# Expert stage of a fused block: gate buffers laid out by blocks of tokens, one gate block built in each step, early inner products split on GpSimd beside the sorting or made from raw weights

## The chip, the cores and the metric

The kernel runs on one core of a Trainium2 chip. A core has five engines that work side by side, each with a queue of its own that it takes in order: TensorE (PE, matrix products, its weight loads shown apart as PEld), VectorE (DVE), ScalarE (ACT), GpSimd (POOL) and SyncE (SP, which issues most of the transfers). The metric is the device time of one execution in microseconds, lower is better. The kernel before takes 1970.99 us, the median of three runs that lie between 1969.98 and 1974.43.

## The reference, cut to what matters

The whole is three layers of a small transformer on 256 tokens of width 1024. The change lies in one stage of it, the expert layer at the end of the first block: 16384 experts, each a row of `u` and a row of `v`. Eight heads choose 16 experts each for every token; a chosen expert gives `gelu(h . u[e]) * g * v[e]`.

```python
q = (hf @ w_q).reshape(n, PEER_HEADS, 2, PEER_HALF)
sc = jnp.einsum('nhcd,hckd->nhck', q, sub_keys)
s_top, i_top = lax.top_k(sc, PEER_TOPK)
cand_s = s_top[:, :, 0, :, None] + s_top[:, :, 1, None, :]
cand_i = i_top[:, :, 0, :, None] * PEER_N_KEYS + i_top[:, :, 1, None, :]
best_s, pos = lax.top_k(cand_s, PEER_TOPK)        # over the 16 x 16 pairs
best_i = jnp.take_along_axis(cand_i, pos, axis=-1)
g = jax.nn.softmax(best_s, axis=-1)
a = jnp.einsum('cd,ced->ce', hc, u[ic])
a = jax.nn.gelu(a, approximate=False) * gc
return jnp.einsum('ce,ced->cd', a, v[ic])
```

All is float32.

## The kernel before, in words

**Products from split weights.** A float32 weight comes from HBM in chunks of 1 MB (`load_ahead`, three buffers called raw). A chunk is cut into pieces of 128 x 1024, and each piece is split into a high and a low part in the format float32r: ACT rounds raw to hi (L287), and another engine subtracts, lo = raw - hi (L289). That engine is VectorE, or GpSimd where the plan says so. `mm3` (L320 to L322) then makes a product as three fast ones: hi x hi, hi x lo, lo x hi. Pieces are split in the order of a plan written out in `plan_peer`, three ahead of their use. There are five buffers each of hi and lo.

**The expert stage** does not gather. It computes all 16384 inner products for all 256 tokens, and multiplies them with a dense table of gates that is zero wherever an expert was not chosen. It goes over 64 steps, `ip`, each with two columns of 128 experts:

- `up(ip)` (from L871): 16 products against the normed input `xT`, split, 128 x 256 each (48 matmuls), then Gelu on ACT (L881) into a buffer `gl`.
- `down(...)`: the gated values times a 1 MB chunk of `v`, 24 matmuls of 128 x 512 each step, all added up in four PSUM banks `po`. Ahead of it a multiply with the gates (L1037, VectorE), a rounding (L1039, ACT) and a difference (L1041, VectorE) give gh and glo.

**The order of the stage.** First the input is normed, transposed and split (`Norm.finish`, `pair`; L385, L386), and the queries (`w_pq`, bank psb) and their scores against the sub-keys (pssc) are made. Then for each tile `t` of 128 tokens comes the sorting on VectorE: `top16` on 16 lists (L919 to L923), the sums of candidate pairs (L933 to L937), `top16` on those; then small operations on 128 x 128 elements that turn positions into pairs of indices (`tu`, `tb`, `fc`, `ab`; L944 to L955), one-hot sums (`eq`, L961 to L966), and the gates IJ (L973). PE transposes IJ (psij, L978), and VectorE casts the result to float16 (`IT`, `JT`, `gT`; L980 to L987).

**The table of gates** is made in quarters of 32 expert columns, in two buffers of [128, 32, 256] by turns. `build(q, n0)` makes 16 tokens of quarter q: one-hot factors on VectorE (oj L997, ei L999, og L1002 twice), 16 matmuls into a bank psg (L1008, twice eight), and for each half of eight tokens a scaled copy on ACT (L1010) and a scaled addition on VectorE (L1011) into the buffer. Their destination is `gates[...][:, :, tokens]` read as (tokens, columns), so neighbouring elements are written 1 KB apart.

**What runs where.** `LEAD` = 20 up-products are made before the main loop: five in the sorting of tile 0, six in that of tile 1, nine beside the 16 builds of quarter 0 (`UPS`). All their 40 pieces have GpSimd for the difference. The first `EARLY` = 10 keep their Gelu results in the second gate buffer, which is free until then; therefore quarter 1 can't be built before step 10, and its 16 builds are packed into steps 10 to 15. Quarters 2 and 3 get one build a step in steps 16 to 47. The other 44 up-products are made in steps 12 to 55, eight steps ahead (`KEEP`).

Apart from the places that fix an order, a scheduler arranges the instructions of each engine at compile time, close to the order of the program.

Of the kernel before, what the change touches and what calls it, by code (L numbers as in the profile page):

```python
# [34 lines left out]
NQ = 4  # L35
# [4 lines left out]
GLO = 2.0 ** 26  # L40
LEAD = 20
UPS = (0, 5, 11)
EARLY = 10
KEEP = LEAD - EARLY - 2
QI = 128 // NQ
# [133 lines left out]
def block_kernel(ctx: ExitStack, tc: tile.TileContext, a: dict, out: bass.AP, start=0, stop=99):  # L179
# [45 lines left out]
    def rsqrt(y, x, mul, add, n):  # L225
        """y = (x * mul + add) ** -0.5"""
# [18 lines left out]

    def plan_chunk(name, off, n, size, eng=None, pieces=None):
        """append pieces of the chunk at off of a weight to the order in which weights are used"""
# [24 lines left out]
            # the first one in parts, to begin with what is there  # L272
# [6 lines left out]
    def split_ahead(upto):  # L279
        """splits pieces of the plan into float32r high and low parts up to the given one"""  # L280
        while done["part"] < min(upto + 1, len(plan)):
# [3 lines left out]
            r = raws[name, off][:, i * size:i * size + w]  # L285
            hi = whi.tile([128, 1024], F32R, name="hi")
            A.activation(out=hi[:, :w], in_=r, func=AF.Copy)  # L287
            lo = wlo.tile([128, 1024], F32R, name="lo")
            eng.tensor_tensor(out=lo[:, :w], in0=r, in1=hi[:, :w].bitcast(F32), op=OP.subtract)  # L289
# [5 lines left out]
    def weights(name, off, ahead=AHEAD):  # L295
        """accessor of a chunk: (column, width) -> high and low parts"""

        def get(c0, n):
# [5 lines left out]
            return hi[:, o:o + n], lo[:, o:o + n]  # L304
# [83 lines left out]
    def transpose_split(src, nk, name, gain=None, pool=None):  # L388
        """src: [128, 2, nk*128] tokens on partitions -> hi, lo [128, nk, 256]"""
# [18 lines left out]
    class Prep:  # L408
        """transposed halves of the residual times a gain, unscaled; the reciprocal root mean square of the tokens apart"""
# [10 lines left out]
        def pair(self, k0):  # L420
# [25 lines left out]
    class Norm(Prep):  # L446
        """scaled before the transposition, which waits for the whole"""
# [5 lines left out]
        def finish(self, pool):  # L453
# [11 lines left out]
    def take(make):  # L465
        """what the stage before has begun, or all of it now"""
# [6 lines left out]
    def begun(make, n):  # L473
        """chunk n of the residual is final: on with what the next stage does to it first"""
# [12 lines left out]
    def ends(nxt, f=add_resid):  # L487
        """consumer of a last product: f, and the beginning of the next stage behind it"""
# [11 lines left out]
    def to_rows(r, pool, name, bank=bank):  # L500
        """[128, 2] per token -> [128, 256], the same on all partitions; made at the first use"""
# [19 lines left out]
    def sin_of(dst, ang, shift, pool, n, nm):  # L521
        """dst = sin(ang + shift * 2 pi), shift in turns; ang [P, n]"""
# [34 lines left out]
    def causal_softmax(pool, ps, nk, bias, scale, e_out, sums):  # L557
        """ps [128, nk] psum scores; e_out [128, nk]; sums [128, 1]"""
# [8 lines left out]
    def transpose_p(pool, p0, p1, name="pT", bank=bank):  # L567
        """p0 [128, 128] (queries 0..127), p1 [128, 256] -> [128, 384]: keys 0..127 x 256 queries, keys 128..255 x queries 128..255"""
# [8 lines left out]
    # ------------------------------------------------------------------ mixing  # L577
# [11 lines left out]
    def mem_kv(p1):  # L589
        """keys and values of the memory"""  # L590
# [23 lines left out]
    def stage_mix():  # L614
        x = prep_mix()
        # in this order: the first products wait for it
# [11 lines left out]
        with ExitStack() as es:  # L628
# [60 lines left out]
            # indexer and selection  # L689
# [21 lines left out]
            # differential attention  # L711
# [40 lines left out]
            # sparse attention  # L752
# [26 lines left out]
            # gates, memory, output  # L779
# [1177 lines left out]
```

## Time and profile before

| | |
|---|---|
| median of three runs | 1970.99 us |
| span of the profiled execution | 1970.1 us |
| PE busy | 1870.6 us, 95% |
| DVE busy | 1464.1 us, 74% |
| ACT busy | 998.0 us, 51% |
| POOL busy | 172.6 us, 9% |
| chain of waits that ended last | PE 82%, DVE 14% |

In the profile a row of a group reads: line, engine, operation, output<-inputs, sizes, count | busy us, mean ns of one | idle time of the engine ahead of it, and what ended that. A row of the timeline reads: start, length, engine, line, operation, count, and in brackets the idle time ahead and what ended it. A row by stretches reads: stretch, its length, busy time of each engine with its number of instructions, granted clock of TensorE, share of the DMA engines, GB/s. Rows of instructions that follow each other overlap a little, and matmuls overlap each other much, so that the distance of their starts is what counts.

### The profile page before, as it was taken

To read this page: it belongs to the slowest core of one execution; us is meant where nothing else is said; L and a number is where in the kernel's file an instruction comes from. 1 tells how busy PE (TensorE), PEld (TensorE's weight loads), DVE (VectorE), ACT (ScalarE), POOL (GpSimd) and SP (SyncE) were. 2 spreads that over 40 slices of the span, in tenths; PEclk is the share of its full clock that TensorE was granted. 3 is DMA by queue.
4 is the path that set the end of the run, shared out by engine and by line. 5 is a ranking of instruction groups with operands and counts; after the bars stand their busy time and mean duration, and the time that the engine had idled before them with its cause. 6 is when DMAs were issued, how large, how long until landed. Compare 5 with 4: busy or idle time off the path is not lost.

```text
span 1970.1 us, 31681 instructions
## 1 busy us (share of the span) xinstructions
PE 1870.6 (95%) x12512; PEld 1659.4 (84%) x12512; DVE 1464.1 (74%) x2893; ACT 998.0 (51%) x1549; POOL 172.6 (9%) x223
## 2 busy tenths in 40 slices
PE   8999989657999999999999999999999999999997
PEld 6777879656878999999999888898899989699996
DVE  7786668999889977887765578641777788677777
ACT  6566456334555555555554454433444466654445
POOL 0000006444000000000000101223000000000000
PEclk9999989878999999999999999998999999999999
DMA  7433424232534555554455544200355545155552
GB/s 275 170 141 112 166 87 157 99 107 86 182 139 152 181 181 175 191 179 172 174 190 184 183 165 147 86 1 12 136 180 193 182 162 180 50 184 193 193 172 96
DMA packets 43766, 296.32 MB, mean 150 GB/s; under 512 B 4897, under 2 KB 5041, under 8 KB 10209
## 3 DMA queue, kind: packets, MB, share of 16 engines
q1 hardware_dynamic: 41872, 289.35, 41.6%
q0 software_dynamic: 1184, 3.89, 0.6%
q8 instruction: 98, 1.61, 0.3%
q10 hardware_dynamic: 560, 1.05, 0.1%
q14 instruction: 52, 0.42, 0.1%
HBM read 293.23 MB, written 1.05 MB: 149 GB/s over the span
## 4 chain that ended last, share of the span: by engine, by line
PE 82%; DVE 14%; ACT 2%; issue 1%; DMA 0%; SPq 0%; ACTq 0%; DVEq 0%
PE po L320 6%; PE po L322 6%; PE po L321 5%; PE psa L321 4%; PE psa L322 4%; PE psa L320 4%; PE psf L320 4%; PE psf L322 4%; PE psf L321 4%; PE acc L321 4%; PE acc L320 4%; PE acc L322 4%; PE psb L320 2%; PE psb L322 2%; PE psb L321 2%; PE go L322 2%
## 5 line engine op out<-in xcount | busy, mean ns | idle before, releaser
L287 ACT ACTIVATE hi<-raw 128x1024 fp32r<-128x1024 f32 (+2 forms) x551 | 575.7, 1047 | 595.3 <-PE psa L321 197.8
L289 DVE TENSOR_TENSOR lo<-raw,hi 128x1024 fp32r<-128x1024 f32 (+3 forms) x511 | 616.7, 1209 | 238.3 <-ACT hi L287 237.7
L322 PE MATMUL psa<-xTh,lo 128*128 128x256 f32 x1024 | 295.0, 288 | 1.9 <-POOL lo L289 1.9
L320 PE MATMUL psa<-xTh,hi 128*128 128x256 f32 x1024 | 295.2, 288 | 0.8 <-ACT hi L287 0.8
L321 PE MATMUL psa<-xTl,hi 128*128 128x256 f32 x1024 | 295.3, 288 | 0.0
L320 PE MATMUL po<-hi,gh 128*128 128x512 f32 x512 | 206.1, 403 | 0.0
L320 PEld LDWEIGHTS psa<-xTh,hi 128*128 128x128 f32 x1024 | 201.5, 197 | 3.0 <-ACT hi L287 1.0
L322 PEld LDWEIGHTS psa<-xTh,lo 128*128 128x128 f32 x1024 | 201.4, 197 | 2.3 <-POOL lo L289 2.1
L321 PEld LDWEIGHTS psa<-xTl,hi 128*128 128x128 f32 x1024 | 201.5, 197 | 1.9
L322 PE MATMUL po<-hi,glo 128*128 128x512 f32 x512 | 202.8, 397 | 0.1
L321 PE MATMUL po<-lo,gh 128*128 128x512 f32 x512 | 202.5, 395 | 0.0
L320 PE MATMUL psf<-xTh,hi 128*128 128x256 f32 x704 | 199.4, 283 | 0.0
L321 PE MATMUL psf<-xTl,hi 128*128 128x256 f32 x704 | 199.2, 283 | 0.0
L322 PE MATMUL psf<-xTh,lo 128*128 128x256 f32 x704 | 198.9, 283 | 0.0
L321 PEld LDWEIGHTS psf<-xTl,hi 128*128 128x128 f32 x704 | 134.6, 191 | 1.8
L320 PEld LDWEIGHTS psf<-xTh,hi 128*128 128x128 f32 x704 | 134.6, 191 | 1.7
L322 PEld LDWEIGHTS psf<-xTh,lo 128*128 128x128 f32 x704 | 134.7, 191 | 0.1
L322 PEld LDWEIGHTS po<-hi,glo 128*128 128x128 f32 x512 | 97.0, 190 | 23.1 <-DVE glo L1041 0.5
L321 PEld LDWEIGHTS po<-lo,gh 128*128 128x128 f32 x512 | 96.8, 189 | 20.2
L320 PEld LDWEIGHTS po<-hi,gh 128*128 128x128 f32 x512 | 96.9, 189 | 20.0
L289 POOL TENSOR_TENSOR lo<-raw,hi 128x1024 fp32r<-128x1024 f32 x40 | 99.5, 2502 | 131.9 <-ACT hi L287 128.6
L321 PE MATMUL acc<-lo,xTh 128*128 128x512 f32 (+3 forms) x288 | 111.0, 385 | 0.0
(635 smaller groups left out, 3690.2 us busy)
## 6 DMA issues: line engine op xcount, KB each, us to landing
raw<-in_u_dram SPq DMA_DIRECT2D x64, 1024.0 KB, 4.8
raw<-in_v_dram SPq DMA_DIRECT2D x64, 1024.0 KB, 4.8
raw<-in_w_f_dram SPq DMA_DIRECT2D x44, 1024.0 KB, 4.9
raw<-in_w_fo_dram SPq DMA_DIRECT2D x22, 1024.0 KB, 4.9
raw<-in_w_in_dram SPq DMA_DIRECT2D x17, 1024.0 KB, 4.8
raw<-in_w_pg_dram SPq DMA_DIRECT2D x8, 1024.0 KB, 4.9
raw<-in_w_hr_dram SPq DMA_DIRECT2D x6, 1024.0 KB, 4.8
raw<-in_w_out_dram SPq DMA_DIRECT2D x4, 1024.0 KB, 4.7
```

Source lines behind the costliest of these rows:

```text
L287: A.activation(out=hi[:, :w], in_=r, func=AF.Copy)
L289: eng.tensor_tensor(out=lo[:, :w], in0=r, in1=hi[:, :w].bitcast(F32), op=OP.subtract)
L320: T.matmul(ps, l[0], r[0], start=first, stop=False, skip_group_check=not check)
L321: T.matmul(ps, l[0], r[1], start=False, stop=False, skip_group_check=not check)
L322: T.matmul(ps, l[1], r[0], start=False, stop=last, skip_group_check=not check)
```

## The change

- Both gate buffers are laid out as [128, 16 blocks, 32 columns, 16 tokens]. Inside a block the tokens of a column lie side by side, so L1010 and L1011 now write runs of eight, and read PSUM with a step of 64 elements (256 bytes) between neighbours.
- Block b of the second buffer holds the Gelu result of up-product b until step b. `EARLY` goes from 10 to 14: blocks 14 and 15 are free from the start, and block b is free after step b. So quarter 1 is built at one block a step in steps 0 to 15, as quarters 2 and 3 are.
- Ten of the 20 early up-products, 5, 6 and 12 to 19 (`RAW`), are made from raw weights: 16 plain float32 matmuls against `x32`, a float32 copy of the normed input, in place of 48. Their pieces are not split at all. `x32` is filled in `pair` by ACT, eight copies more at the start of the stage. Its place is later taken by `gx`, the pairs gh and glo.
- `UPS` becomes (0, 7, 14): seven up-products beside each tile's sorting, six (all raw) beside the builds of quarter 0.
- The first GpSimd split that is planned after the sorting of tile 0 has been written out waits for the last small cast of that tile (`gate`).
- `SLOTS` = 9 Gelu buffers instead of 10, `KEEP` = 7 steps ahead instead of 8; up-products 20, 21 and 22 come in steps 4, 8 and 12, the others in steps 16 to 56 (`UP_AT`).
- The one-hot tensors `irep` and `eq` have one buffer in place of two; `irep` lies in the place of the queries.

```diff
-UPS = (0, 5, 11)
-EARLY = 10
-KEEP = LEAD - EARLY - 2
+UPS = (0, 7, 14)
+RAW = {5, 6, 12, 13, 14, 15, 16, 17, 18, 19}
+EARLY = 14
+SLOTS = 9
+KEEP = SLOTS - 2
+UP_AT = {4 * (n - LEAD) + 4: [n] for n in range(LEAD, EARLY + SLOTS)}
+UP_AT.update({n - KEEP: [n] for n in range(EARLY + SLOTS, 64)})
...
 def split_ahead(upto):
...
+            if eng == "raw":
+                parts[done["part"]] = r, None
+                chunks["left"][name, off] -= 1
+                done["part"] += 1
+                continue
...
-            eng.tensor_tensor(out=lo[:, :w], in0=r, in1=hi[:, :w].bitcast(F32), op=OP.subtract)
+            ins = eng.tensor_tensor(out=lo[:, :w], in0=r, in1=hi[:, :w].bitcast(F32), op=OP.subtract)
+            if eng is G and gate:
+                tc.add_manual_dep(ins.ins, gate.pop().name, mybir.DependencyInfo(mybir.DependencyClass.Sync, mybir.DependencyReason.DATA), reason="pause")
...
 def pair(self, k0):
...
+                if self.full is not None:
+                    A.activation(out=self.full[:, k0 + j, :], in_=ps[:, j * 256:(j + 1) * 256], func=AF.Copy, scale=self.gain(k0 + j))
...
-            gelu_p = es.enter_context(pool("pegl", LEAD - EARLY))
-            gates = [None, p0.tile([128, QI, 256], F32, name="gate1")]
+            gelu_p = es.enter_context(pool("pegl", SLOTS))
+            gates = [None, p0.tile([128, NB, QI, 256 // NB], F32, name="gate1")]
+            x32 = p0.tile([128, 8, 256], F32, name="x32", tag="x32")
...
-                        mm3(ps[:, m * 256:(m + 1) * 256], uw((m * 8 + k) * 128, 128),
-                            (xT[0][:, k, :], xT[1][:, k, :]), k == 0, k == 7)
+                        w = uw((m * 8 + k) * 128, 128)
+                        if ip in RAW:
+                            T.matmul(ps[:, m * 256:(m + 1) * 256], w[0], x32[:, k, :], start=k == 0, stop=k == 7)
+                        else:
+                            mm3(ps[:, m * 256:(m + 1) * 256], w, (xT[0][:, k, :], xT[1][:, k, :]), k == 0, k == 7)
...
-                    V.tensor_scalar(out=gT[1][:, ts], in0=gf, scalar1=GLO / GHI, scalar2=None, op0=OP.mult)
+                    small = V.tensor_scalar(out=gT[1][:, ts], in0=gf, scalar1=GLO / GHI, scalar2=None, op0=OP.mult)
+                    if t == 0:
+                        gate.append(small.ins)
...
-                    d = gates[q % 2][:, :, n0 + b * nb:n0 + (b + 1) * nb].rearrange("p i n -> p n i")
-                    A.activation(out=d, in_=ps[:, :, 0], func=AF.Copy, scale=1.0 / GHI)
-                    V.scalar_tensor_tensor(out=d, in0=ps[:, :, 1], scalar=1.0 / GLO, in1=d, op0=OP.mult, op1=OP.add)
+                    d = gates[q % 2][:, n0 // NB, :, b * nb:(b + 1) * nb]
+                    A.activation(out=d, in_=ps[:, :, 0].rearrange("p n i -> p i n"), func=AF.Copy, scale=1.0 / GHI)
+                    V.scalar_tensor_tensor(out=d, in0=ps[:, :, 1].rearrange("p n i -> p i n"), scalar=1.0 / GLO, in1=d, op0=OP.mult, op1=OP.add)
...
+            gx = p0.tile([128, 2, 2, 2, 256], F32R, name="gx", tag="x32")
             for ip in range(NP):
-                if LEAD <= ip + KEEP < NP:
-                    up(ip + KEEP)
+                for n in UP_AT.get(ip, ()):
+                    up(n)
                 q, i0 = divmod(2 * ip, QI)
                 if q + 1 < NQ:
-                    f0 = EARLY if q == 0 else 0
-                    b0, b1 = (max(0, x - f0) * 16 // (16 - f0) for x in (i0 // 2, i0 // 2 + 1))
-                    for b in range(b0, b1):
-                        build(q + 1, b * NB)
+                    build(q + 1, (ip + EARLY) % NB * NB if q == 0 else ip % NB * NB)
...
-                V.tensor_tensor(out=g, in0=g, in1=gates[q % 2][:, i0:i0 + 2, :], op=OP.mult)
-                gh = ge.tile([128, 2, 256], F32R, name="gh", tag="gh")
+                g4 = g.rearrange("p m (b n) -> p m b n", b=NB)
+                V.tensor_tensor(out=g4, in0=g4, in1=gates[q % 2][:, :, i0:i0 + 2, :].rearrange("p b i n -> p i b n"), op=OP.mult)
+                gh, glo = gx[:, ip % 2, 0], gx[:, ip % 2, 1]
...
-            plan_chunk("u", ip * 128 * 2048, 2048, 1024, G)
+            plan_chunk("u", ip * 128 * 2048, 2048, 1024, "raw" if ip in RAW else G)
```

More of the change, by code (lines that the diff above doesn't have):

```diff
@@ L244, in block_kernel @@
     done = {"raw": 0, "part": 0}
+    gate = []
     def plan_chunk(name, off, n, size, eng=None, pieces=None):
@@ L303, in get @@
             hi, lo = parts[p]
-            return hi[:, o:o + n], lo[:, o:o + n]
+            return hi[:, o:o + n], lo[:, o:o + n] if lo is not None else None
         return get
@@ L408, in block_kernel @@
     class Prep:
+        full = None
         def __init__(self, gain, src=None, bank=bank, pool=hT):
@@ L451, in chunk, with finish @@
                 self.square(t, n)
-        def finish(self, pool):
+        def finish(self, pool, full):
+            self.full = full
             r = self.rstd()
@@ L885, in stage_peer @@
                 p1 = es2.enter_context(pool("pe1", 1))
-                p2 = es2.enter_context(pool("pe2", 2))
-                xT = take(prep_peer).finish(p1)
+                xT = take(prep_peer).finish(p1, x32)
                 sk = p1.tile([128, 8, 128], F32, name="sk")
@@ L891, in stage_peer @@
                 V.tensor_copy(ia, iof[:, 0:16].unsqueeze(2).to_broadcast([128, 16, 16]))
-                qT = p1.tile([128, 8, 256], F32, name="pqT")
+                qT = p1.tile([128, 8, 256], F32, name="pqT", tag="pqT")
                 scs = [p1.tile([128, 2, 8, 128], F32, name=f"psc{t}", tag=("xs", "psc1")[t]) for t in range(2)]
@@ L956, in stage_peer @@
                     IJ = p1.tile([128, 3, 8, 16], F32, name="IJ", tag="IJ")
+                    irep = p1.tile([128, 2, 8, 16, 16], BF, name="irep", tag="pqT")
                     for c in range(2):
-                        rp_ = p2.tile([128, 8, 16, 16], BF, name="irep", tag="irep")
+                        rp_ = irep[:, c]
                         A.copy(out=rp_, in_=ib[:, c].unsqueeze(3).to_broadcast([128, 8, 16, 16]))
-                        eq = p2.tile([128, 8, 16, 16], BF, name="eq", tag="eq")
+                        eq = p1.tile([128, 8, 16, 16], BF, name="eq", tag="eq")
                         V.tensor_tensor(out=eq, in0=ab[:, c].rearrange("p (h s) -> p h s", s=16).unsqueeze(2).to_broadcast([128, 8, 16, 16]),
@@ L986, in stage_peer @@
                     V.tensor_tensor(out=gf, in0=gf, in1=gT[0][:, ts], op=OP.subtract)
-                    V.tensor_scalar(out=gT[1][:, ts], in0=gf, scalar1=GLO / GHI, scalar2=None, op0=OP.mult)
+                    small = V.tensor_scalar(out=gT[1][:, ts], in0=gf, scalar1=GLO / GHI, scalar2=None, op0=OP.mult)
+                    if t == 0:
+                        gate.append(small.ins)
             oh = es.enter_context(pool("peo", 2))
-            ge = es.enter_context(pool("pee", 2))
             gp = es.enter_context(pool("peg", 1))
-            gates[0] = gp.tile([128, QI, 256], F32, name="gate0")
+            gates[0] = gp.tile([128, NB, QI, 256 // NB], F32, name="gate0")
             def build(q, n0):
@@ L1047, in stage_peer @@
                     tail.pop()
-            last = ends(lambda: Both(gates[0][:, 0:4, :].rearrange("p a n -> p (a n)")))
+            last = ends(lambda: Both(gates[0][:, 0:2].rearrange("p b i n -> p (b i n)")))
             for hf in range(2):
@@ L1882, in plan_peer @@
         for ip in range(LEAD):
-            plan_chunk("u", ip * 128 * 2048, 2048, 1024, G)
+            plan_chunk("u", ip * 128 * 2048, 2048, 1024, "raw" if ip in RAW else G)
         for ip in range(64):
-            if LEAD <= ip + KEEP < 64:
-                plan_chunk("u", (ip + KEEP) * 128 * 2048, 2048, 1024)
+            for n in UP_AT.get(ip, ()):
+                plan_chunk("u", n * 128 * 2048, 2048, 1024)
             plan_chunk("v", ip * 128 * 2048, 2048, 1024)
```

5 lines of the change are left out of this document (2 added, 3 removed).

## The prediction

> **What bounds the kernel now.** I read the profile page first, then the busy time by stretches of the expert stage, then the timelines of VectorE (DVE), GpSimd (POOL) and TensorE (PE) inside those stretches.
>
> ```profile
> span 1970.1 us, 31681 instructions
> ...
> core 0: us, PE busy (x) PEld busy (x) DVE busy (x) ACT busy (x) POOL busy (x), PEclk, DMA share, GB/s
> 320.00:366.00 46.00, 31.97 (x252) 31.45 (x251) 46.00 (x176) 21.14 (x22) 24.37 (x11) 0.85 0.32 115
> 366.00:415.40 49.40, 32.56 (x245) 31.63 (x244) 48.53 (x178) 19.76 (x22) 26.07 (x11) 0.83 0.36 129
> 415.40:495.40 80.00, 60.15 (x596) 57.98 (x596) 74.32 (x102) 34.52 (x53) 35.21 (x13) 0.87 0.26 88
> 505.60:561.40 55.80, 55.80 (x242) 45.06 (x241) 37.88 (x43) 26.44 (x31) 0.00 (x0) 1.00 0.53 189
> 561.40:637.50 76.10, 68.92 (x593) 58.59 (x593) 73.55 (x110) 41.75 (x61) 0.00 (x0) 0.98 0.39 139
> 637.50:1150.90 513.40, 513.29 (x3577) 461.45 (x3577) 380.26 (x467) 262.02 (x332) 10.47 (x31) 1.00 0.51 179
> ```
>
> The rows are, in order: sorting of token tile 0, sorting of tile 1, the 16 builds of gate quarter 0, steps 0 to 9 of the main loop, steps 10 to 15 (in which all of quarter 1 is built), steps 16 to the end. PE is full in steps 0 to 9 and from step 16 on. DVE is full, and PE idle for a quarter to a third, in the three stretches before the loop, and again in steps 10 to 15. So the stage has two kinds of time: 569 us that only less PE work would shorten, and 252 us that are DVE's. POOL is busy in just the first three rows.
>
> ```profile
> 356.45 0.69 PE L978 MATMUL psij<-ident,IJ 128*128 128x128 f32 x2 [13.54 <-DVE IJ L966]
> ...
> 412.46 0.69 PE L978 MATMUL psij<-ident,IJ 128*128 128x128 f32 x2 [13.84 <-DVE IJ L966]
> ...
> 330.13 19.04 POOL L289 TENSOR_TENSOR lo<-raw,hi 128x1024 fp32r<-128x1024 f32 x8 [6.73 <-ACT hi L287]
> ...
> 332.62 2.45 DVE L944 TENSOR_SCALAR tu<-pu 128x128 uint32<-128x128 uint32 x1
> ...
> 349.17 0.21 DVE L955 TENSOR_TENSOR ab<-ab,fc 128x128 bf16<-128x128 bf16 x1
> ...
> 357.31 0.27 DVE L973 TENSOR_TENSOR IJ<-gd,gs 128x128 f32<-128x128 f32 x1
> ...
> 364.67 1.25 DVE L985 CAST gT<-gf 128x128 f16<-128x128 f32 x1
> ...
> 366.51 2.29 DVE L987 TENSOR_SCALAR gT<-gf 128x128 f16<-128x128 f32 x1
> ...
> 388.60 2.40 DVE L944 TENSOR_SCALAR tu<-pu 128x128 uint32<-128x128 uint32 x1
> ...
> 405.04 0.21 DVE L953 TENSOR_TENSOR ab<-ab,fc 128x128 bf16<-128x128 bf16 x1
> 405.17 0.21 DVE L955 TENSOR_TENSOR ab<-ab,fc 128x128 bf16<-128x128 bf16 x1
> ...
> 415.39 1.22 DVE L997 TENSOR_TENSOR oj<-JT,io 128x2048 f16<-128x2048 f16 x1
> ```
>
> Each tile's sorting ends in small operations (L944 to L955), whose results PE waits for, 13.5 and 13.8 us. Operations of 128 elements take 2.3 to 2.45 us there, the length of one GpSimd split (19.04/8 = 2.38). The same kind takes 0.21 us the moment POOL's eight splits end, at 349.17. DVE is not working in these rows; it waits its turn behind each GpSimd split. Seven operations pay: 332.62 to 349.17 in tile 0 and 388.60 to 405.04 in tile 1, 16.5 us each, which without splits beside them are 7 x 0.2 = 1.4.
>
> **The builds** pay too. By line, busy time in the builds of quarter 0, then in a stretch of the main loop without GpSimd (oj first, then og):
>
> ```profile
> 415.39:495.43 80.04, 25.16 (x17) 0.87 0.26 88
> 700.00:800.00 100.00, 10.83 (x9) 1.00 0.51 180
> ...
> 415.39:495.43 80.04, 24.32 (x34) 0.87 0.26 88
> 700.00:800.00 100.00, 6.02 (x16) 1.00 0.51 180
> ```
>
> oj: 25.16 - 17 x 1.203 = 4.7 us lost; og: 24.32 - 34 x 0.376 = 11.5. Together 16.
>
> **The change, part by part.** Prices on PE first: one split up-product (48 matmuls), ten down-products (240), and plain float32 matmuls of 256 columns, which the raw products will be made of.
>
> ```profile
> 577.20:582.96 5.76, 5.72 (x48) 5.70 (x48) 0.00 (x0) 1.00 0.80 313
> ...
> 505.60:561.30 55.70, 55.67 (x240) 45.06 (x240) 0.00 (x0) 1.00 0.53 189
> ...
> 261.61 1.90 PE L847 MATMUL mo<-mpT,mv 128*128 128x256 f32 x8
> ```
>
> A split product is 5.76 us, a down step 5.57. The eight float32 matmuls start 1.9/8 = 0.22 to 0.24 us apart, so a raw product (16) is 3.5 us, and one raw product saves 2.3 us of PE.
>
> The Trainium skill (FP8 and Floating Point Precision, section TensorE Precision Notes) has true float32 as four passes through the array. By that the raw products would be no cheaper than the split ones, and the row just quoted, at about two passes' worth, speaks against it; the sum goes by the row, the other price is the second rival.
>
> *Start of the stage.* Eight more ACT copies (x32) stand between the eight hi parts that the query products wait for:
>
> ```profile
> 282.34 2.33 ACT L385 ACTIVATE xTh<-pst,cols 128x256 fp32r<-128x256 f32 x6 [0.17 <-PE pst L425]
> ...
> raw<-in_u_dram SPq DMA_DIRECT2D x64, 1024.0 KB, 4.8
> ```
>
> 0.39 us each, 3.1 in all; the first 48 products run on half of the parts and hide most. I take +1 (0 to 3).
>
> *Tile 0.* Products 0 to 4 still split on GpSimd, 5 and 6 are raw. Of the eight splits in a row, three (the rest of 3 and 4) still run, until about 337.3. Splits for product 7 need the buffer that product 4 frees: 337.3 + 4.8 landing + about 1 for ACT = 343, so DVE has some 6 us alone. Two or three splits then meet the one-hot operations behind. I keep four collisions of 2.25 us: of 15.1 in the seven operations and 3 at L985 and L987, 9 go, 9 stay (bounds: 0 to 18 go). PE: products 0 to 4 ended at 356.45 - 13.54 = 342.9; +1, and two raw (7.0) give 351; DVE's IJ comes at 357.3 + 1 - 7 = 351. Neither waits long.
>
> *Tile 1.* A new wait holds GpSimd's split queue until the last small cast of tile 0 (L987). Behind it are seven splits, of products 8 to 11, and nothing else; PE's products wait for them. The cast comes at about 360 (9 us behind IJ as before, its collision gone), so the seven end at 360 + 7 x 2.4 = 377. Between IJ and the small operations lay 388.6 - 357.6 = 31 us; without 3 us of collisions at the casts they begin 28 behind 351, at 379. All 15.1 us go (bounds: 0 and 15.1). PE: from 352.5, five split (28.8) and two raw (7) products: 388.3, where DVE's IJ comes at about 389 (379 + 1.4 + the 8 us from 349.2 to 357.3 in tile 0). Raw products hold one of three load buffers until PE has read it: the load for product 8 waits for product 5 (347.5) and lands with 4.8 at 352, six us ahead of its use. The builds begin at 415.4 + 1 - 9 - 15.1 = 392.3.
>
> *Builds of quarter 0.* No GpSimd split is left: 80.0 - 16 = 64. PE has six raw products in it, 21 us, hidden in the quarter of the stretch that it idles and in the three split products' worth that it no longer makes; their loads, ten us apart, hide as well. The pair gh and glo takes the place of x32, so the first rounding waits for the last raw product: nothing while that is hidden, 3.5 us if it comes last. The new layout is the open price:
>
> ```profile
> L1011 DVE SCALAR_TENSOR_TENSOR gate<-psg,gate 128x256 f32<-128x256 f32 x128 | 84.1, 708 | 13.2 <-ACT gate L1010 12.7
> L1602 DVE SCALAR_TENSOR_TENSOR c<-g,cols,c 128x256 f32<-128x256 f32 x44 | 21.1, 484 | 4.0
> L1010 ACT ACTIVATE gate<-psg 128x256 f32<-128x256 f32 x128 | 68.9, 653 | 37.0 <-PE psg L1008 37.0
> L382 ACT ACTIVATE loTh<-mlo 128x256 fp32r<-128x256 f32 x8 | 3.1, 384 | 6.8 <-PE mlo L1857 6.8
> ```
>
> The two gate operations write single elements a kilobyte apart and cost 0.22 and 0.27 us more than contiguous ones of their size. Afterwards they write runs of eight, but read PSUM 256 bytes apart, which no row shows. Bounds on DVE: 32 x 0.22 = 7 us less, or as much more. I take half of the gain, 3.5: 60.5 us, ending at 453.
>
> The Trainium skill (Advanced Engine Details and Errata, section Memory Cachelines) asks for neighbouring accesses in both memories, with a line of 16 bytes in SBUF and 8 in PSUM. So it has the writes gain and the reads lose; the rows agree on the writes, none shows the reads.
>
> *Main loop.* PE's work from the first down-product on is unchanged: 64 x 5.57 + 44 x 5.76 + 48 builds. The builds' share is what is left of steps 16 on: (513.4 - 48 x 5.57 - 40 x 5.76)/32 = 0.49 us. In all 633.4. Before it began at 505.6, 10 us behind DVE since up-products were still queued, and lost 76.1 - (6 x 5.57 + 4 x 5.76 + 16 x 0.49) = 11.8 in steps 10 to 15. Now no product is queued, but four operations of a build, a multiply and two roundings come first, about 5 us: it begins at 458. Steps 0 to 15 then have a build each:
>
> ```profile
> L289 DVE TENSOR_TENSOR lo<-raw,hi 128x1024 fp32r<-128x1024 f32 x489 | 597.0, 1223 | 230.2 <-ACT hi L287 229.7
> L1037 DVE TENSOR_TENSOR gl<-gl,gate 128x512 f32<-128x512 f32 x54 | 36.1, 685 | 0.0
> L999 DVE TENSOR_TENSOR ei<-IT,io 128x512 f16<-128x512 f16 x64 | 27.2, 437 | 0.0
> L1041 DVE TENSOR_TENSOR glo<-gl,gh 128x512 fp32r<-128x512 f32 x54 | 37.2, 690 | 15.2 <-ACT gh L1039 15.1
> ```
>
> DVE per step: two splits 2.4, L1037 and L1041 1.4, one build 3.8 (1.2 + 0.44 + 2 x 0.38 + 2 x 0.71), 7.6 summed, about 6.8 since a row starts 0.08 before its forerunner ends (405.04 and 405.17 above; ten rows). Sixteen steps and three products' splits (2.3 each): 116 (129 without overlap). PE: 16 x 6.06 + 3 x 5.76 = 114. They nearly tie; I allow a loss of 4 (0 to 12) in place of 11.8. L1037 reads its gates in runs of 16 from now on, which I price at nothing: beyond step 16 PE covers it, and in these steps 0.1 us of it would be 1.6. One slot and one step less of lead for the up-products costs nothing where PE is full. Behind a DVE that ties, the gate operations' saving counts again, inside these 4. The loop ends at 458 + 633.4 + 4 = 1095.4, against 1150.9.
>
> *Sum:* +1 - 9 - 15.1 - 19.5 (builds) - 5 (backlog 10 against 5) - 8 (steps 10 to 15) = -55.6. On the span: 1970.1 - 55.6 = 1914.5; the median of the runs, 1970.99, is 0.9 above the span, so **1915**.
>
> **The rivals.**
>
> *The gate opens late* (0.18). If the cast of tile 0 comes behind 362, the held splits run into the small operations of tile 1 again. For it: the margin above is 2 us, and L987 stood 9 us behind IJ because DVE's order put sorting ahead of it. Price up to 15: 1915 to 1930, say 1925.
>
> *Raw products cost double* (0.05): 16 x 0.44 = 7 us. PE then bounds both sortings, +7 each, less 1 of slack: 1928. The row of eight speaks against it.
>
> *DVE bounds steps 0 to 15* (0.10): without overlap 129 against 114, and every wait of DVE for ACT on top; loss 12 to 20 instead of 4: 1923 to 1931.
>
> *The strided PSUM read is dear, and the kernel slower* (0.04). A gate operation of x us costs 64 x (x - 0.71) on DVE in the builds of quarter 0 and steps 0 to 15; the gain of 56 and the 3.5 within it are overtaken at x = 1.6. At 1.9: 64 x 1.19 + 3.5 = 80 more than forecast, 1995. The present 0.71 with a stride on the write makes more than twice that unlikely.
>
> *The change moves nothing* (0.01): it would need PE to be the bound before 495, which its 13.5 and 13.8 us of waiting deny.
>
> **How the numbers follow.** The forecast has 0.62; all but one of its rivals are faster too. Low end: all 18 of tile 0 go (-9), the whole layout gain and no loss in steps 0 to 15 (-7.5), no start cost (-1): 1897. High end: tile 0 gains nothing (+9), tile 1 half (+8), the loop loses 12 (+8), no layout gain (+3.5): 1943. The range is 1896 to 1943. Runs of this kernel differ by about 0.2% (4 us), the bound for "same". Faster 0.95 (0.62 + 0.18 + 0.05 + 0.10), same 0.01, slower 0.04.
>
> **What would show it.** Right: no run of 2.3 us rows in L944 to L955 of tile 1; POOL idle behind about 380, 20 splits instead of 40; oj and og at 1.2 and 0.38 in the builds; the first down-product near 458; PE full from there but for a few us. Raw products 3.5 us long. Wrong: POOL rows over tile 1's small operations (first rival); PE idle behind psij no longer, but DVE waiting for it (second); DVE over 97% busy with PE gaps through steps 0 to 15 (third); L1011 far above 0.7 us (fourth).

## The result, and the profile after

The changed kernel takes 1927.63 us (median of four runs, 1924.75 to 1929.50) against 1970.49 for the kernel before (1968.48 to 1974.43): a ratio of 0.9778, with a 95% interval of 0.9761 to 0.9795. It is faster by 43 us, where 56 were forecast. The profiled execution, the fastest of the four, has this span and these busy times on its page:

```profile
span 1923.0 us, 31276 instructions
...
PE 1865.4 (97%) x12352; PEld 1649.0 (86%) x12352; DVE 1402.7 (73%) x2893; ACT 952.5 (50%) x1537; POOL 123.4 (6%) x203
```

PE is now busy for 97% of the span. Where the 47 us of span went shows in the busy time by stretches. First the changed kernel: sorting of tile 0, sorting of tile 1, builds of quarter 0 up to the first down-product, main loop.

```profile
core 0: us, PE busy (x) PEld busy (x) DVE busy (x) ACT busy (x) POOL busy (x), PEclk, DMA share, GB/s
318.70:364.70 46.00, 45.86 (x332) 43.95 (x330) 46.00 (x227) 18.70 (x20) 18.11 (x8) 1.00 0.38 138
364.70:414.80 50.10, 37.85 (x241) 35.96 (x242) 36.67 (x124) 16.81 (x19) 17.58 (x7) 0.86 0.31 108
414.80:466.10 51.30, 49.26 (x442) 42.06 (x440) 51.30 (x106) 18.53 (x43) 0.00 (x0) 1.00 0.38 139
466.10:1106.10 640.00, 639.95 (x4423) 567.71 (x4424) 478.59 (x635) 312.18 (x431) 11.26 (x31) 1.00 0.51 179
```

The last two stretches, cut the same way, in the kernel before:

```profile
415.40:505.60 90.20, 70.35 (x681) 68.18 (x681) 84.52 (x116) 39.85 (x59) 35.21 (x13) 0.89 0.27 94
505.60:1154.50 648.90, 641.61 (x4426) 567.96 (x4424) 494.76 (x625) 333.81 (x431) 10.47 (x31) 1.00 0.49 174
```

The builds begin 0.6 us earlier than before (414.8 against 415.4), so the sorting has gained nothing. From there to the first down-product it is 51.3 us instead of 90.2, and the main loop takes 640.0 instead of 648.9, with PE full. That is 48.4 us up to the last down-product; the rest of the span is 1.3 longer.

**The sorting.** PE's timeline shows the two raw products of tile 0 and the transposition behind them:

```profile
341.38 13.98 PE L900 MATMUL psa<-x,raw 128*128 128x256 f32 x64
355.20 0.49 PE L1005 MATMUL psij<-ident,IJ 128*128 128x128 f32 x3
```

Two products are 64 instructions, so each of their 16 matmuls is two. They fill 341.38 to 355.20: 6.9 us a product, where 3.5 was forecast and a split product takes 5.76. In GpSimd's timeline the held splits begin behind tile 0's last cast:

```profile
374.56 7.06 POOL L303 TENSOR_TENSOR lo<-raw,hi 128x1024 fp32r<-128x1024 f32 x3 [17.02 <-DVE gT L1014]
382.65 10.52 POOL L303 TENSOR_TENSOR lo<-raw,hi 128x1024 fp32r<-128x1024 f32 x4 [1.04 <-ACT hi L301]
```

PE's timeline shows who paid:

```profile
376.95 0.58 PE L338 MATMUL psa<-xTh,lo 128*128 128x256 f32 x1 [12.39 <-POOL lo L303]
377.33 0.41 PE L336 MATMUL psa<-xTh,hi 128*128 128x256 f32 x1
377.55 0.41 PE L337 MATMUL psa<-xTl,hi 128*128 128x256 f32 x1
...
381.77 0.28 PE L336 MATMUL psa<-xTh,hi 128*128 128x256 f32 x1
381.89 0.28 PE L337 MATMUL psa<-xTl,hi 128*128 128x256 f32 x1
```

The wait cost PE more than its 12.4 us: behind it, from 377.2 to 381.6, the granted clock is 0.50 and the matmuls start 0.21 us apart instead of 0.12, which is 2.2 us more.

The last cast was expected at about 360; VectorE's timeline has it at 374:

```profile
372.68 0.27 DVE L1007 CAST IT<-psij 128x128 f16<-128x128 f32 x1
374.18 0.21 DVE L1014 TENSOR_SCALAR gT<-gf 128x128 f16<-128x128 f32 x1
377.33 2.05 DVE L995 TENSOR_TENSOR gd<-best 128x128 f32<-128x128 f32 x1
379.30 2.40 DVE L970 TENSOR_SCALAR tu<-pu 128x128 uint32<-128x128 uint32 x1
...
382.75 2.44 DVE L979 TENSOR_TENSOR ab<-ab,fc 128x128 bf16<-128x128 bf16 x1
385.11 2.44 DVE L981 TENSOR_TENSOR ab<-ab,fc 128x128 bf16<-128x128 bf16 x1
387.47 3.44 DVE L988 TENSOR_TENSOR eq<-ab,ia 128x2048 bf16<-128x2048 bf16 x1
...
400.24 0.29 DVE L993 TENSOR_TENSOR IJ<-eq 128x128 f32<-128x128 bf16 x1
413.38 0.29 DVE L1007 CAST IT<-psij 128x128 f16<-128x128 f32 x1 [12.85 <-PE psij L1005]
414.83 1.22 DVE L1025 TENSOR_TENSOR oj<-JT,io 128x2048 f16<-128x2048 f16 x1
```

PE had transposed tile 0 at 355.2, but DVE came to it only at 372.7, without having been idle: tile 1's sorting stood ahead of it in its order. So the pause ended just as tile 1's small operations began, and four of those of 128 elements again took 2.05 to 2.44 us beside the splits. The last row but one is new: DVE has its IJ at 400.5 and waits 12.85 us for PE. Before, PE waited for DVE there. PE's side adds up: from 355.6 on, five split products (28.8 us) and two raw ones (13.8) would have ended at 398.2, just ahead of DVE; with 12.4 us of waiting and the 2.2 of the low clock it is 412.8, and PE transposes tile 1 at 413.1.

**The builds.** The groups of the changed kernel that belong to them, over the whole run:

```profile
L1025 DVE TENSOR_TENSOR oj<-JT,io 128x2048 f16<-128x2048 f16 x64 | 78.1, 1220 | 34.3 <-PE psg L1036 34.3
L1030 DVE TENSOR_TENSOR og<-ei,gT 128x512 f16<-128x512 f16 x128 | 48.7, 416 | 0.0
L1039 DVE SCALAR_TENSOR_TENSOR gate<-psg,gate 128x256 f32<-128x256 f32 x128 | 48.1, 417 | 1.8 <-ACT gate L1038 1.2
L1038 ACT ACTIVATE gate<-psg 128x256 f32<-128x256 f32 x128 | 41.6, 379 | 22.8 <-PE psg L1036 22.6
```

The two gate operations fell from 708 and 653 ns to 417 and 379. ACT's 379 are what it takes for this size in one run (384, L382 in the prediction), so reading PSUM 256 bytes apart costs nothing that shows. The price had been the single elements a kilobyte apart, which both engines wrote and DVE also read.

### The profile page after: what moved, and what is told of

It reads as the page before. It is cut to its first block, busy times and chain, and to the rows that moved or that the text cites. A ratio compares the mean times of both kernels' runs of the same rounds, so it can differ in the third digit from the quotient of the medians.

```text
span 1923.0 us, 31276 instructions
## 1 busy us (share of the span) xinstructions
PE 1865.4 (97%) x12352; PEld 1649.0 (86%) x12352; DVE 1402.7 (73%) x2893; ACT 952.5 (50%) x1537; POOL 123.4 (6%) x203
## 4 chain that ended last, share of the span: by engine, by line
PE 87%; DVE 10%; ACT 2%; issue 1%; DMA 0%; POOL 0%; SPq 0%; ACTq 0%; POOLq 0%; DVEq 0%
PE po L336 6%; PE po L337 6%; PE po L338 6%; PE psa L338 5%; PE psa L336 5%; PE psa L337 5%; PE psf L336 4%; PE psf L338 4%; PE psf L337 4%; PE acc L337 4%; PE acc L338 4%; PE acc L336 4%; PE psb L336 2%; PE go L338 2%; PE psb L338 2%; PE psb L337 2%
## 5 line engine op out<-in xcount | busy, mean ns | idle before, releaser
L301 ACT ACTIVATE hi<-raw 128x1024 fp32r<-128x1024 f32 (+3 forms) x531 | 554.2, 1046 | 575.6 <-PE psa L337 142.5
L338 PE MATMUL psa<-xTh,lo 128*128 128x256 f32 x864 | 245.5, 284 | 12.4 <-POOL lo L303 12.4
L337 PE MATMUL psa<-xTl,hi 128*128 128x256 f32 x864 | 245.4, 284 | 0.0
L336 PE MATMUL psa<-xTh,hi 128*128 128x256 f32 x864 | 245.4, 284 | 0.0
L336 PE MATMUL po<-hi,gx 128*128 128x512 f32 x512 | 206.9, 404 | 2.1 <-ACT gx L1067 2.1
L337 PE MATMUL po<-lo,gx 128*128 128x512 f32 x512 | 203.2, 397 | 0.0
L338 PE MATMUL po<-hi,gx 128*128 128x512 f32 x512 | 200.6, 395 | 0.0
L338 PEld LDWEIGHTS psa<-xTh,lo 128*128 128x128 f32 x864 | 166.6, 193 | 12.7 <-POOL lo L303 12.6
L337 PEld LDWEIGHTS psa<-xTl,hi 128*128 128x128 f32 x864 | 166.5, 193 | 1.9
L336 PEld LDWEIGHTS po<-hi,gx 128*128 128x128 f32 x512 | 97.0, 189 | 23.1 <-ACT gx L1067 3.2
L338 PEld LDWEIGHTS po<-hi,gx 128*128 128x128 f32 x512 | 96.8, 189 | 22.6
L337 PEld LDWEIGHTS po<-lo,gx 128*128 128x128 f32 x512 | 97.1, 190 | 20.1
L336 PE MATMUL acc<-hi,xTh 128*128 128x512 f32 (+3 forms) x288 | 110.4, 385 | 0.3 <-ACT hi L301 0.3
```

The source lines that it names most:

```text
L336: T.matmul(ps, l[0], r[0], start=first, stop=False, skip_group_check=not check)
L337: T.matmul(ps, l[0], r[1], start=False, stop=False, skip_group_check=not check)
L338: T.matmul(ps, l[1], r[0], start=False, stop=last, skip_group_check=not check)
```

## The experiments

The theory after this result was: the gain is the layout and the builds without splits beside them; the sorting lost its gain to the place of the pause. The main rivals: the layout is worth little; a pause costs at any place; PE, through its 6.9 us raw products, bounds the sorting whatever the pause does. All times are medians, each ratio is against the kernel before, run beside it on the same chip (medians of 1972.08 to 1973.19 us for the runs from e1_layout on). The last three columns are from the profiled executions: first operation of the builds, first and last down-product.

| run | us | ratio (95%) | builds | first | last |
|---|---|---|---|---|---|
| before | 1970.49 | | 415.4 | 505.6 | 1154.5 |
| after | 1927.63 | 0.9778 (0.9761 to 0.9795) | 414.8 | 466.1 | 1106.1 |
| e1_layout | 1959.03 | 0.9929 (0.9909 to 0.9948) | 414.6 | 501.6 | 1141.8 |
| e2_steps | 1955.17 | 0.9910 (0.9892 to 0.9927) | 415.4 | 504.0 | 1141.4 |
| e3_no_gate | 1929.43 | 0.9777 (0.9756 to 0.9799) | 417.6 | 468.9 | 1107.5 |
| e4_gate_early | 1925.78 | 0.9765 (0.9745 to 0.9785) | 418.0 | 469.3 | 1108.0 |
| e5_raw6 | 1935.65 | 0.9815 (0.9799 to 0.9832) | 425.7 | 476.9 | 1116.9 |
| e6_raw_builds | 1932.12 | 0.9797 (0.9781 to 0.9814) | 402.6 | 476.1 | 1113.0 |
| e7_all_raw | 1920.25 | 0.9733 (0.9716 to 0.9750) | 411.3 | 462.5 | 1102.5 |
| e8_four_loads | 1930.34 | 0.9790 (0.9774 to 0.9806) | 422.6 | 473.8 | 1112.0 |
| e9_raw16 | 1918.84 | 0.9721 (0.9708 to 0.9734) | 409.1 | 462.1 | 1102.0 |
| e10_dve6 | 1922.78 | 0.9748 (0.9735 to 0.9761) | 414.8 | 466.1 | 1106.1 |
| e11_copies | 1919.67 | 0.9736 (0.9718 to 0.9755) | 411.4 | 462.7 | 1102.8 |
| e12_copies_four | 1925.97 | 0.9764 (0.9746 to 0.9783) | 420.5 | 471.7 | 1109.9 |

No edit is made to the part of the program behind the last down-product (only e8_four_loads and e12_copies_four have other numbers of buffers there), yet that part takes 813.9 to 819.9 us in these executions. A difference between two times that the last column does not show lies there and can't be put down to the edit.

**The layout alone.** The kernel before with the change's gate buffers:

```diff
-gates[0] = gp.tile([128, QI, 256], F32, name="gate0")
+gates[0] = gp.tile([128, NB, QI, 256 // NB], F32, name="gate0")
...
-d = gates[q % 2][:, :, n0 + b * nb:n0 + (b + 1) * nb].rearrange("p i n -> p n i")
+d = gates[q % 2][:, n0 // NB, :, b * nb:(b + 1) * nb]
```

> The kernel before with the new layout of the gate buffers and nothing else. Theory (the layout is a main part of the gain): the gate operations fall from 0.71 and 0.65 us to about 0.42 and 0.38; 32 of them on DVE save 9 us in the builds of quarter 0, and 32 in steps 10 to 15 take most of the 11.8 us that PE loses there: 1951 to 1956, 15 to 19 us under the kernel before. Rival (the layout is worth little, and the builds of quarter 0 shortened because GpSimd's splits left them): the gate operations are shorter, but splits on GpSimd and waits for PE fill the room: 1965 or more.

Measured: 1959.03, 14 us under the kernel before on its chip (1973.19), 12.7 of them up to the last down-product. Its gate group on DVE, and its builds and main loop by stretches:

```profile
L1011 DVE SCALAR_TENSOR_TENSOR gate<-psg,gate 128x256 f32<-128x256 f32 x128 | 47.6, 417 | 6.2 <-ACT gate L1010 5.7
```

```profile
414.60:501.60 87.00, 69.41 (x682) 67.12 (x682) 80.75 (x117) 33.48 (x59) 36.00 (x13) 0.89 0.27 97
501.60:1141.80 640.20, 638.76 (x4426) 566.85 (x4424) 471.51 (x624) 312.26 (x431) 10.46 (x31) 1.00 0.49 177
```

The main loop has all that it has in the changed kernel, 640.2 us, still with quarter 1 built in steps 10 to 15. In the builds of quarter 0 its 32 gate operations are 9 us shorter together (32 x 0.29), but the stretch shortened by only 3.2 and DVE's busy time by 3.8 (84.52 to 80.75). The splits on GpSimd are still beside it there, 36.0 us of them, and take most of the rest back at another operation: the 18 of ei last 13.3 us in this stretch, where they lasted 8.2 in the kernel before. The time lies between the two expectations.

**The even steps alone**, added to that:

```diff
-EARLY = 10
-KEEP = LEAD - EARLY - 2
+EARLY = 14
+SLOTS = 9
...
-    for b in range(b0, b1):
-        build(q + 1, b * NB)
+    build(q + 1, (ip + EARLY) % NB * NB if q == 0 else ip % NB * NB)
```

> As e1_layout, and with one build of quarter 1 in each of steps 0 to 15 instead of all 16 in steps 10 to 15, with the buffers and the loading order that belong to it; all 20 early products are still split on GpSimd. Theory: e1_layout has already taken most of the loss in steps 10 to 15, so the even spread adds 2 to 5 us of gain, and the backlog of products in front of the first down-product another 0 to 5: 1945 to 1952. Rival (the even spread is worth what the prediction gave the whole main loop, 8 us, whatever the layout): 8 or more below e1_layout. If neither, the lesser room for early results costs: e1_layout or above.

Measured: 1955.17. The intervals of e1_layout and e2_steps overlap (from 0.9909 to 0.9927), and the last down-product comes only 0.4 us earlier: the spread is worth 4 us by the medians and perhaps nothing. Its builds still take 88.6 us. The rest of the way to 1927.63 must come from the raw products, from what they take off GpSimd, and from the order that goes with them.

**The wait taken out, and the wait moved.**

```diff
-                    if t == 0:
-                        gate.append(small.ins)
```

> The changed kernel without the wait of GpSimd's split for the cast of tile 0. Theory (the pause is what tile 1 loses by: PE idles 12.4 us for the first held split, and the held splits then run beside the small operations): without it the splits run from the moment their buffers come free, tile 1's products are early, and 10 to 13 us go: 1914 to 1918. Rival (PE is the bound of the sorting by its 6.8 us raw products, or the splits meet the small operations at another place): 1924 or more.

```diff
-gate.append(small.ins)
+gate.append(ij.ins)
```

> The changed kernel with the wait moved from tile 0's last cast to tile 0's last sorting operation (the product IJ, which PE transposes), 17 us earlier in DVE's order. Theory (the place of the wait costs, not the wait): the held splits end before tile 1's small operations begin, PE does not wait for them: 10 to 14 us under the changed kernel, at or a little below e3_no_gate: 1913 to 1918. Rival (a pause at any place costs PE its products): between e3_no_gate and the changed kernel, 1922 or more.

(ij is the operation that writes IJ[:, 2], at L1000.) Measured: 1929.43 and 1925.78, both intervals overlapping the changed kernel's. Neither the wait nor its place is worth anything that shows; the theory of the place fell. In e4_gate_early no split waits for the gate any more, and the timelines of the two are alike. PE's 12.4 us in one piece became 9.9 in five pieces in e3_no_gate (engine and line, releaser, total us, times, longest):

```profile
ACT hi L301 <- DMA raw<-in_u_dram: 24.6, 3, 10.1
...
PE psa L338 <- POOL lo L303: 5.2, 3, 2.5
...
PE psa L336 <- ACT hi L301: 4.7, 2, 2.6
```

The low clock took back what was won: it follows two of these pieces, 4.3 and 4.9 us at 0.50, so that PE loses 4.6 us by it in place of 2.2. Something else was late next, and the loads were the first suspect, since a raw product holds its load buffer until PE has read it.

**Four load buffers**, and DVE in place of ACT for the copies irep, each with and without the other. All runs from here on leave the wait in GpSimd's queue out.

```diff
-RAWS = 3
+RAWS = 4
...
-SLOTS = 9
+SLOTS = 8
...
-    wraw = ctx.enter_context(tc.tile_pool(name="wraw", bufs=3))
-    whi = ctx.enter_context(tc.tile_pool(name="whi", bufs=5))
-    wlo = ctx.enter_context(tc.tile_pool(name="wlo", bufs=5))
+    wraw = ctx.enter_context(tc.tile_pool(name="wraw", bufs=4))
+    whi = ctx.enter_context(tc.tile_pool(name="whi", bufs=4))
+    wlo = ctx.enter_context(tc.tile_pool(name="wlo", bufs=4))
```

> e3_no_gate with four load buffers instead of three (paid for with one buffer less each of the high and low parts and of the early results). Theory (with the wait gone, PE's 10 us of waiting in the sorting is for loads, since a raw product holds its load buffer until PE has read it): most of it goes, 1917 to 1922. Rival (the splits are late because of ACT's order or GpSimd's pace): no change against e3_no_gate, 1926 or more; the lesser buffers may also cost other stages.

Measured: 1930.34, no change against e3_no_gate; the last down-product comes 4.5 us later. ACT's waits for loads in the sorting fell from 24.6 us to 4.4 and nothing was won, so PE's waits were not the loads' alone. ACT's timeline in e8_four_loads, and a wait of PE:

```profile
352.53 0.60 ACT L908 ACTIVATE gate<-psa 128x512 f32<-128x512 f32 x1 [3.09 <-PE psa L900]
376.85 3.70 ACT L986 COPY irep<-ib 128x2048 bf16<-128x2048 bf16 x2 [23.73 <-DVE ib L955]
...
380.94 1.04 ACT L301 ACTIVATE hi<-raw 128x1024 fp32r<-128x1024 f32 x1
```

```profile
PE psa L336 <- ACT hi L301: 10.0, 1, 10.0
```

ACT stood 23.7 us in front of a copy that needs tile 1's sorted indices, with the rounding that PE waited for behind it. So the next pair:

```diff
-A.copy(out=rp_, in_=ib[:, c].unsqueeze(3).to_broadcast([128, 8, 16, 16]))
+V.tensor_copy(out=rp_, in_=ib[:, c].unsqueeze(3).to_broadcast([128, 8, 16, 16]))
```

> e3_no_gate (no wait in GpSimd's queue) with the copies irep made by DVE instead of ACT. The first theory of the load buffers fell with e8_four_loads; the theory now is that ACT's order took the wait's place: the roundings hi of the next products stand behind the copies irep of tile 1, which wait for DVE's sorting. Theory: with the copies gone from ACT, some of PE's 10 us of waits goes, as far as the loads allow, 1921 to 1927; DVE pays 2 to 5 us for the copies, which its 15 us of waiting for PE hide. Rival (loads are what is late, through three buffers): 1928 or more.

> e8_four_loads (no wait, four load buffers) with the copies irep made by DVE instead of ACT. Theory (in e8_four_loads the loads had landed and PE waited 10 us at one place for roundings that stood behind the copies in ACT's queue): that wait goes, 1918 to 1923, and below e11_copies. Rival (the exponential of tile 1, which also stands ahead of roundings on ACT and waits for DVE, or the splits running into the small operations, takes the place once more): 1927 or more.

Measured: 1919.67 with three load buffers, 10 us under e3_no_gate and more than expected. Only 4.7 of them show at the last down-product; the rest is behind the stage, where e3_no_gate's execution takes 819.9 us and this one 813.9. With four it is 1925.97, 4 us under e8_four_loads with intervals that overlap, so there the rival's "takes the place once more" is nearer than the theory. The waits of e11_copies in the sorting name the successor:

```profile
ACT gd L996 <- DVE gd L995: 22.7, 2, 16.2
...
PE psa L336 <- ACT hi L301: 5.5, 1, 5.5
PE psa L338 <- POOL lo L303: 1.7, 1, 1.7
```

PE's 9.9 us became 7.2, with one stretch at the low clock behind them instead of two, and what stands on ACT ahead of a rounding is now the exponential of tile 1 (L996), which waits 16.2 us for DVE. In e3_no_gate it had already stood there, with 5.1 us. The builds begin 6.2 us earlier. The fourth buffer did not help in either pair. It was paid for with buffers of other kinds, so these runs do not say what a fourth alone would do.

**Where the raw products are needed.** Beside the builds alone, with less and less in the sorting:

```diff
-UPS = (0, 7, 14)
-RAW = {5, 6, 12, 13, 14, 15, 16, 17, 18, 19}
+UPS = (0, 5, 11)
+RAW = {11, 12, 13, 14, 15, 16, 17, 18, 19}
```

> e3_no_gate with the first 11 products split on GpSimd and the last 9 raw, and the transpositions after products 0, 5 and 11 as before the change: raw products beside the builds alone. It is e2_steps with raw products 11 to 19 instead of split ones. Theory (the builds of quarter 0 shorten because no split runs beside them, which needs nothing of the sorting): the builds are then bound by PE, 9 x 6.8 + 8 = 69 us, the first down-product comes 478 to 488 instead of 504, and the time is 1929 to 1939, 16 to 26 under e2_steps. Rival (the gain beyond e2_steps comes from the sorting): within 6 us of e2_steps, 1949 or more.

Measured: 1932.12, 23 us under e2_steps, from which it also differs by the single buffers of irep and eq. The builds up to the first down-product in e2_steps and in e6_raw_builds:

```profile
415.40:504.00 88.60, 69.58 (x697) 67.38 (x697) 80.57 (x119) 33.97 (x60) 34.85 (x13) 0.88 0.27 96
```

```profile
402.60:476.10 73.50, 72.74 (x573) 62.79 (x571) 64.96 (x129) 20.79 (x49) 0.00 (x0) 0.99 0.36 130
```

Without splits beside them DVE's work in the builds falls from 80.6 to 65.0 us, and PE, with nine raw products, becomes the bound: 72.7 of 73.5. The sorting, with 7 splits in tile 1 instead of 12, ends 12.8 us earlier. Most of what the change gains beyond layout and steps is here, with no raw product and no pause in the sorting.

```diff
-RAW = {5, 6, 12, 13, 14, 15, 16, 17, 18, 19}
+RAW = {14, 15, 16, 17, 18, 19}
```

> e3_no_gate with products 5, 6, 12 and 13 split on GpSimd again; raw are only 14 to 19, beside the builds. Theory (a raw product costs PE 1.1 us more than a split one, 6.8 against 5.76, and GpSimd's splits cost DVE 2.3 us for each small operation that they meet, and in the sorting the one just pays for the other): the builds begin within 4 us of where they do in e3_no_gate, the time is 1924 to 1932. Rival (PE alone bounds the sorting): four times 1.1 us and the 10 us that PE waits for loads in e3_no_gate go, 1915 to 1920. Other rival (collisions return in full): 1938 or more.

Measured: 1935.65, 6 us above e3_no_gate (9.4 at the last down-product), between the theory's band and the second rival's. The builds begin 8 us later than in e3_no_gate, with 21 splits in two long rows over the sorting, and in both tiles somebody waits:

```profile
332.22 26.17 POOL L303 TENSOR_TENSOR lo<-raw,hi 128x1024 fp32r<-128x1024 f32 x11 [6.79 <-ACT hi L301]
389.98 23.72 POOL L303 TENSOR_TENSOR lo<-raw,hi 128x1024 fp32r<-128x1024 f32 x10 [31.59 <-ACT hi L301]
```

```profile
ACT irep L986 <- DVE ib L955: 32.3, 2, 30.1
...
PE psij L1005 <- DVE IJ L993: 11.1, 2, 6.5
PE psa L336 <- ACT hi L301: 8.6, 1, 8.6
```

So the four raw products of the sorting do earn something. **All twenty raw**, and GpSimd out of it:

```diff
-RAW = {5, 6, 12, 13, 14, 15, 16, 17, 18, 19}
+RAW = set(range(20))
```

> e3_no_gate with all 20 early products raw: no split on GpSimd at all, and no other product changed. Theory (once raw, the stretch from the first product to the first down-product is PE's: 20 x 6.8 + 8 = 144 us without a pause, as long as the changed kernel takes with 10 raw products and its waits): 1923 to 1932, PE full, DVE waiting for PE before the builds. Rival (DVE and its collisions with GpSimd bound the stretch to the end): 10 us or more below the changed kernel, 1917 or less. If raw products wait for loads beyond their 6.8 us: 1936 or more.

Measured: 1920.25; its interval (0.9716 to 0.9750) lies below the changed kernel's. PE in the sorting, one wait, and DVE's last sorting operation of tile 1 in e7_all_raw:

```profile
318.70:414.80 96.10, 96.10 (x450) 84.48 (x450) 63.70 (x354) 21.30 (x24) 0.00 (x0) 1.00 0.42 154
```

```profile
DVE IT L1007 <- PE psij L1005: 32.1, 1, 32.1
```

```profile
377.45 0.29 DVE L993 TENSOR_TENSOR IJ<-eq 128x128 f32<-128x128 bf16 x1
```

PE is never idle, and its granted clock is 1.00 throughout, where it is 0.93 over the same stretch in the changed kernel. DVE has finished tile 1 at 377.7 instead of 400.5, 23 us earlier, and then waits 32 us for PE. Free of GpSimd, the sorting is PE's, as the theory said; the time is 3 us under its band, since the ten more raw products cost PE less, 10 x 1.15 = 11.5 us, than its wait with the low clock behind it had, 14.6.

Two attempts to buy PE time back followed:

```diff
-RAW = set(range(20))
+RAW = set(range(4, 20))
```

> e7_all_raw with products 0 to 3 split on GpSimd, in the time in which the queries' scores are still made, and the other 16 raw. Theory (in e7_all_raw PE is full from the first product on and every raw product costs it 1.04 us more than a split one, while the splits of the first four end before the small operations of tile 0): 3 to 5 us under e7_all_raw, 1915 to 1918. Rival (the splits' ends, the rounding on ACT and the collisions on DVE give it back): e7_all_raw or above, 1920 or more.

```diff
-RAW = set(range(4, 20))
+RAW = {4, 5, 12, 13, 14, 15, 16, 17, 18, 19}
...
-            plan_chunk("u", ip * 128 * 2048, 2048, 1024, "raw" if ip in RAW else G)
+            plan_chunk("u", ip * 128 * 2048, 2048, 1024, "raw" if ip in RAW else G if ip < 4 else V)
```

> e9_raw16 with products 6 to 11 split on DVE, which waits 32 us for PE before the builds in e7_all_raw; raw are 4, 5 and 12 to 19. Theory (DVE's 12 splits at 1.2 us fit into these 32 us, no operation waits behind them, and PE saves 6 x 1.04 us): 5 to 7 us under e9_raw16, 1908 to 1912. Rival (the splits or their rounding on ACT stand behind the sorting in these engines' order and PE waits for them, as it did for the roundings behind the copies in e8_four_loads): above e9_raw16 by 3 us or more.

Measured: 1918.84, which can't be told from e7_all_raw (1920.25); the builds begin 2.2 us earlier, the first down-product 0.4. And 1922.78 with six products split on DVE: 4 us slower, as the rival said. DVE still waits 20 us for PE there, and PE waits for roundings and splits:

```profile
PE psa L336 <- ACT hi L301: 7.3, 1, 7.3
...
PE psa L338 <- DVE lo L303: 3.0, 1, 3.0
```

DVE's 20 spare us lie at the end of the sorting; its splits were needed in the middle. e7_all_raw, e9_raw16 and e11_copies beat both kernels of this case and can't be told from each other.

## Why the prediction was right, and where its steps failed

The direction and the range held, and that it came so near is luck: 1915 is 12.6 us from the median, 1914.5 is 8.5 from the span of the profiled execution (1923.0), and errors of 22.5 us too much in the sorting and 15.3 too little behind it cancelled in part. By stretches:

| step | forecast | measured |
|---|---|---|
| start and sorting, to the first build | -23.1 | -0.6 |
| builds and backlog, to the first down-product | -24.5 | -38.9 |
| main loop | -8 | -8.9 |
| all, to the last down-product | -55.6 | -48.4 |

- **The raw product, 3.5 us, was mis-sized: 6.9.** The quoted row of "eight float32 matmuls 0.22 to 0.24 us apart" was read as eight matmuls of the program. L900 shows that a float32 matmul is two instructions, 32 for the 16 matmuls of a product, so the row had four; L847 itself has 8 matmuls in the program and 16 instructions in the trace of the kernel before. One matmul of 256 columns costs 13.82/32 = 0.43 us, 3.6 times the 0.12 (5.76/48) of a float32r one. This failed step made "one raw product saves 2.3 us of PE" into one that costs 1.1 more. The Trainium skill's rule of four passes for true float32 (FP8 and Floating Point Precision, TensorE Precision Notes), which the prediction set aside for the row, is near the measured price of 3.6 passes; the row had been counted wrongly.
- **Start, +1.** PE waits 0.9 us for x32 ahead of the first query product, and no more.
- **Tile 0, -9 and "neither waits long".** PE reached the transposition at 355.2 instead of 351. The same term, 6.8 us more for two raw products, covers that; without it PE would have been a little early.
- **Tile 1, "the cast comes at about 360".** It came at 374.2. The "9 us behind IJ as before" was taken from a kernel in which DVE was the late one; here PE was, DVE went on with tile 1's sorting meanwhile and came back 17 us later. This is the first rival (0.18), and the price of the second (0.05) came with it: PE was forecast to be through at 388.3 and was at 413.1, 9.9 us of that by the raw products of both tiles (3.1 left from tile 0, 6.8 in tile 1), 12.4 by the wait and 2.2 by the low clock. But the first rival's price was not its own: without the wait (e3_no_gate) as much time is lost to roundings that stand in ACT's order behind copies and an exponential, which wait for DVE. Moving the copies (e11_copies) or all raw (e7_all_raw) is what brings 3 to 5 us up to the last down-product, and 7 to 10 by the medians.
- **The collisions** were seen rightly as a mechanism: without a split (e7_all_raw) DVE ends its sorting at 377.7, 23 us earlier than in the changed kernel and 35 earlier than in the kernel before, where PE's transposition at 412.46 waited for it; the upper bounds of the two tiles were 18 and 15.1, 33.1 together. The step that was missing is PE's: it had been 13 us early in each tile and with 6.9 us raw products was no longer.
- **Builds, 60.5 us.** The 16 us of collisions were right: by the groups of this stretch oj fell from 25.2 to 20.7 us and og from 24.4 to 12.7. The half of the layout's gain, taken as a middle between unknowns, was all of it, 0.29 us for each gate operation (9.2 us for 3.5), and DVE's 5.7 us of waiting in that stretch (74.32 of 80), which the sum left standing without a reason, went too. Beside the builds the raw products' double price was nearly hidden: the stretch is 51.3 us for DVE and 49.3 for PE. The Trainium skill (Advanced Engine Details and Errata, Memory Cachelines) asks that every two consecutive elements be neighbours in PSUM; ACT's 379 ns with a 256-byte stride, against 384 in one run, show no price for it here.
- **Main loop, -8.** Right in size. It was argued from the even spread of the builds; e1_layout, without the spread, has the same 640 us loop, so the layout is enough for it. On top of the layout the spread is worth 4 us by the medians and 0.4 up to the last down-product; the spread without the layout was not run.
- DVE bounding steps 0 to 15 and a dear PSUM read did not happen: PE is busy 639.95 of 640.00 us in the loop.

Not tried: a fourth load buffer with nothing taken away; the exponential moved out of the roundings' way, whose price is therefore not shown.

## What to carry to other kernels

When a wait is removed and nothing moves, look down the in-order queues of the engines in between: here three different things (a pause on GpSimd, copies on ACT, an exponential on ACT) stood ahead of the same work, and the last two showed fully only once the pause was gone. Count a wait of PE with the low clock behind it: several short waits can cost as much as one long one. Price an instruction from a row only after counting how many instructions the program's operation becomes, best against a product whose number of matmuls is known. And where an engine that slows another has only a little work left, try giving it none: the simplest variant, with every early product raw, beat the carefully mixed one by 7 us, 3.6 of them up to the last down-product.

## What the runs showed of the hardware

- A float32 matmul (128x128 by 256 columns) is two instructions 0.216 us apart: 6.9 us for 16 of them, against 5.76 for the same product as 48 float32r ones. Besides, it needs no rounding, no split and no GpSimd.
- Behind a wait of 12.4 us PE's granted clock was 0.50 for 4.4 us, and its matmuls started 0.21 us apart instead of 0.12. In e3_no_gate, behind pieces of 1.9 to 2.6 us, it was 0.50 for 4.3 and 4.9 us. With PE never idle (e7_all_raw) it stayed at 1.00 through the sorting.
- Beside a GpSimd split of 2.4 us the bf16 one-hot operations of 128x2048 took 3.1 to 3.4 us instead of 1.2, and several of those of 128x128 took 2.05 to 2.45 instead of the 0.2 to 0.3 that they take in e7_all_raw.
- Output in single elements a kilobyte apart costs ACT 0.27 us for 128x256 float32, and DVE, which also reads them so, 0.29; reading PSUM with a stride of 256 bytes and writing runs of eight costs nothing that shows (ACT 379 ns, against 384 in one run).
